# Alternating heavy and light experts, boundary tiles in pieces, the experts' sum in PSUM, light blocks in pairs

## The chip, the cores and the metric

The kernel runs on one NeuronCore of a Trainium2 chip. The core has TensorE (PE, matrix products, with its own weight loads), VectorE (DVE), ScalarE (ACT) and GpSimd (POOL); SyncE (SP) issues the weights' transfers from the chip's memory to 16 DMA engines. The metric is the time of one execution on the device in microseconds, the median of several runs. All numbers below are us unless marked otherwise.

## The reference

Two layers run over 256 tokens of width 1024. Each has a mixing sublayer (gated DeltaNet and MoBA attention, merged and projected by `w_o`) and a channel mixer: dense SwiGLU of width 2816 in layer 0, and in layer 1 eight SwiGLU experts of width 3584, of which each token uses two. After each sublayer the stream is normalised.

```python
mix = jnp.einsum('bsd,de->bse', g_a * y_a + g_b * y_b, w_o[layer])
x = _layer_norm(DEEPNORM_ALPHA * x + mix, ln1_g[layer], ln1_b[layer])
...
if layer % 2 == 0:
    ffn = _swiglu(x, ffn_w_gate[i], ffn_w_up[i], ffn_w_down[i])
else:
    ffn = _moe_swiglu(x, router_w[i], router_b[i], exp_w_gate[i], exp_w_up[i], exp_w_down[i])
x = _layer_norm(DEEPNORM_ALPHA * x + ffn, ln2_g[layer], ln2_b[layer])
...
for e in range(N_EXPERTS):
    y = y + gates[..., e:e + 1] * _swiglu(x, w_gate[e], w_up[e], w_down[e])
```

The last loop is that of `_moe_swiglu`; `gates` holds the softmax of each token's two largest router logits and is zero elsewhere. Everything is float32.

## The kernel before, in words

*Weights.* All large weights come in tiles of 128x2048 float32 (1 MB), in the order in which they are used. Class `Weights` loads a tile through SP (L76) into a raw slot, and splits it for PE into a high part `wh` (ACT, a copy to fp32r, L81) and a low part `wl` (DVE, raw minus high, L82); each has three buffers. The MoE phase has ten raw slots, among them `xhr`, `xlr`, `hbr`, `ohlr`, taken from tiles that are no longer used. A product is made as three matmuls per step of k (L205 to L207: high by high, low by high, high by low). A wait on a tile's conversion can be attached to a layer norm by `W.after`; `W.low` sends a tile's low half to another engine: at each of the three layer boundaries (`mix_out` of both layers, and `dense`) the next two tiles' low halves go to GpSimd.

*Boundaries.* The layer norm (`layer_norm_`, L236 to L260) runs for two halves of the tokens (c = 0, 1). For each half DVE makes statistics and two steps (L244, L245) per 512 columns, PE transposes the result (L250), and ACT and DVE write the transposed halves `xh` and `xl` (L253, L254). Ahead of the MoE the result is also kept untransposed as high and low part, `nat`: ACT L259, GpSimd L260. Behind it comes the router: PE L849, DVE L850 to L905, among which a rank of the experts by their number of tokens.

*Experts.* Each expert has 42 tiles: 28 for gate and up, two per block of 256 hidden units (14 blocks), and 14 for down. Tokens are gathered by matmuls with one-hot matrices (`onehot`, `gather`: PE L973, ACT L979, DVE L981), in groups of experts (0), (1, 2), (3, 4), (5, 6), (7), at the end of the last expert of the group before. A *heavy* expert holds up to 128 tokens and takes three matmuls per k (`tm`). A *light* one has up to 64: its high and low parts stand side by side in the 128 columns, so that two matmuls per k do (`tml`, L1027), and a fold by a matrix on PE (L1014) adds the halves. Three experts are heavy (the first three in order of their number of tokens), then five light ones.

A light block is worked on by `light_act`: ACT evicts the 128x512 result (L1011), PE folds (L1014, into `dl1`), ACT makes the silu (L1016), DVE the product (L1017, 128x128), ACT the high part (L1018), DVE the low part (L1019). A heavy block goes through `ffn_act` (L746 to L752, 128x256).

After the down product ACT and DVE make the gated result's high and low part (`ohl`, L1073, L1074), PE scatters it back to the tokens by one-hot matrices (L1079, L1080), and DVE adds it to `y` in four pieces of 128x512 (L1083), for all experts but the last, whose sum is made in PSUM with y.

*PSUM.* There are eight banks: `aux`, `mo`, `pm` twice each, `dl0`, `dl1` once. Gate and up results rotate through pm, pm, dl0; down uses the two of aux; gather, gates, one-hot transposes and the scatter use mo.

*Order.* A scheduler orders the instructions of each engine by the dependences and by the order of the code, with its own estimates; each engine then runs its list in order.

## Time and profile before

| | us |
|---|---|
| runs: median (lowest to highest of 3) | 1821.34 (1819.23 to 1824.04) |
| profiled execution | 1824.69 |
| its span | 1822.9 |
| PE busy in the span | 1738.2 |
| PE weight load | 1449.9 |
| DVE busy | 1389.8 |
| ACT busy | 1219.3 |
| POOL busy | 153.9 |

Busy times are sums over the span. Within it the mixing layers and the dense part take about the first half (the router ends near 890), and the eight experts follow, 101 to 126 us each. Which engine fills a stretch differs from stretch to stretch, so the share of the span says little by itself. An arrow behind a row in the views below, as in `[4.21 <-DVE res L245]`, tells how long the engine stood idle before that row, and what it waited for.

### The profile page before, as it was taken

What the parts mean: (1) busy time and instruction counts of PE and PEld (TensorE: products, weight loads), DVE (VectorE), ACT (ScalarE), POOL (GpSimd) and SP (SyncE); (2) the same over time, 40 slices, a digit from 0 to 9 for tenths busy, and PEclk for the clock granted to TensorE, in tenths of its full rate; (3) what the DMA queues carried; (4) which work ended last, traced back from release to release, by engine and by line L of the source; (5) the groups of instructions that cost most, each with busy time, mean ns of one, the idle gap of its engine ahead of it and who ended that gap; (6) DMA issues with size and microseconds to landing.
All of it is one profiled execution on the core that took longest, in us unless ns stands there. A gap on an engine that the chain in (4) does not pass through costs nothing.

```text
span 1822.9 us, 25299 instructions
## 1 busy us (share of the span) xinstructions
PE 1738.2 (95%) x9628; PEld 1449.9 (80%) x9628; DVE 1389.8 (76%) x1417; ACT 1219.3 (67%) x1363; POOL 153.9 (8%) x303
## 2 busy tenths in 40 slices
PE   8999999899989999999799999999999999999996
PEld 7988998788869888998678888888777767677774
DVE  5665556655455665547798888988999999999997
ACT  5676564444436656653477777777898889889895
POOL 0133200200020332201210000000000000000000
PEclk9999999999999999999799999999999999999998
DMA  8444334455544543337679999999999999999993
GB/s 274 169 147 137 113 131 177 178 184 185 184 162 162 165 152 115 110 116 289 265 276 346 350 352 369 347 362 348 391 410 410 414 411 408 421 394 421 418 407 126
DMA packets 100894, 492.13 MB, mean 270 GB/s; under 512 B 22099, under 2 KB 37916, under 8 KB 44060
## 3 DMA queue, kind: packets, MB, share of 16 engines
q1 hardware_dynamic: 72544, 475.91, 68.2%
q10 hardware_dynamic: 28220, 14.52, 2.9%
q8 instruction: 78, 1.28, 0.3%
q14 instruction: 52, 0.43, 0.1%
HBM read 484.61 MB, written 5.78 MB: 269 GB/s over the span
## 4 chain that ended last, share of the span: by engine, by line
PE 61%; DVE 15%; issue 7%; ACT 6%; POOL 6%; DMA 4%; ACTq 0%; DVEq 0%; SPq 0%; POOLq 0%
DVE wl L82 10%; PE pm L206 8%; PE pm L207 8%; PE pm L205 8%; ACT wh L81 4%; PE pm L1027 4%; PE aux L205 4%; PE aux L207 4%; PE aux L206 4%; POOL bLU L451 3%; POOL bT L449 3%; PE dl L1027 2%; PE dl L205 2%; PE dl L206 2%; PE dl L207 2%
## 5 line engine op out<-in xcount | busy, mean ns | idle before, releaser
L82 DVE TENSOR_TENSOR wl<-wraw,wh 128x2048 fp32r<-128x2048 f32 (+1 forms) x389 | 851.0, 2197 | 238.5 <-ACT wh L81 233.2
L81 ACT ACTIVATE wh<-wraw 128x2048 fp32r<-128x2048 f32 (+1 forms) x394 | 722.8, 1840 | 260.3 <-PE dl L207 48.5
L205 PE MATMUL pm<-xh,wh 128*128 128x256 f32 x896 | 263.2, 294 | 2.1 <-ACT wh L81 1.5
L207 PE MATMUL pm<-xh,wl 128*128 128x256 f32 x896 | 262.1, 293 | 1.1 <-DVE wl L82 1.1
L206 PE MATMUL pm<-xl,wh 128*128 128x256 f32 x896 | 262.3, 293 | 0.0
L205 PEld LDWEIGHTS pm<-xh,wh 128*128 128x128 f32 x896 | 172.5, 193 | 8.8 <-issue 4.8
L207 PEld LDWEIGHTS pm<-xh,wl 128*128 128x128 f32 x896 | 172.6, 193 | 6.2 <-issue 3.4
L206 PEld LDWEIGHTS pm<-xl,wh 128*128 128x128 f32 x896 | 172.5, 192 | 6.2 <-issue 4.8
L1027 PE MATMUL pm<-wl,xgh 128*128 128x512 f32 x376 | 157.2, 418 | 9.0 <-DVE wl L82 8.1
L1027 PE MATMUL pm<-wh,xgh 128*128 128x512 f32 x376 | 149.3, 398 | 0.4 <-ACT sg L1011 0.4
L1027 PE MATMUL aux<-wl,hb 128*128 128x512 f32 x280 | 106.9, 420 | 8.7 <-DVE wl L82 5.2
L1027 PEld LDWEIGHTS pm<-wl,xgh 128*128 128x128 f32 x376 | 70.9, 189 | 40.0 <-DVE wl L82 26.5
L1027 PE MATMUL aux<-wh,hb 128*128 128x512 f32 x280 | 99.3, 394 | 0.0
L206 PE MATMUL pm<-wl,xgh 128*128 128x512 f32 x224 | 90.5, 404 | 2.6 <-DVE wl L82 2.6
L205 PE MATMUL pm<-wh,xgh 128*128 128x512 f32 x224 | 91.9, 411 | 0.0
L207 PE MATMUL pm<-wh,xgl 128*128 128x512 f32 x224 | 89.8, 402 | 0.0
L1027 PEld LDWEIGHTS aux<-wl,hb 128*128 128x128 f32 x280 | 52.5, 187 | 43.9 <-DVE wl L82 34.3
L1027 PEld LDWEIGHTS pm<-wh,xgh 128*128 128x128 f32 x376 | 70.9, 189 | 13.9 <-ACT sg L1011 0.8
L1027 PE MATMUL dl<-wl,xgh 128*128 128x512 f32 x184 | 76.7, 417 | 5.2 <-DVE wl L82 4.8
L82 DVE TENSOR_TENSOR wl<-xhr,wh 128x2048 fp32r<-128x2048 f32 (+1 forms) x36 | 75.7, 2111 | 4.1 <-ACT wh L81 4.0
L1014 PEld LDWEIGHTS dl<-fold,sg 128*128 128x128 f32 x560 | 73.1, 191 | 6.0
L82 DVE TENSOR_TENSOR wl<-xlr,wh 128x2048 fp32r<-128x2048 f32 x32 | 73.3, 2289 | 4.1 <-ACT wh L81 3.6
(436 smaller groups left out, 3491.9 us busy)
## 6 DMA issues: line engine op xcount, KB each, us to landing
wraw<-in_w_exp SPq DMA_DIRECT2D x260, 1024.0 KB, 7.3
wraw<-in_w_mix SPq DMA_DIRECT2D x77, 1024.0 KB, 4.9
wraw<-in_w_ffn SPq DMA_DIRECT2D x33, 1024.0 KB, 4.8
xlr<-in_w_exp SPq DMA_DIRECT2D x33, 1024.0 KB, 7.2
xhr<-in_w_exp SPq DMA_DIRECT2D x32, 1024.0 KB, 7.1
LU<-zLU ACTq DMA_DIRECT2D x8, 512.0 KB, 3.9
hbr<-in_w_exp SPq DMA_DIRECT2D x4, 1024.0 KB, 10.9
wraw<-in_w_exp SPq DMA_DIRECT2D x12, 256.0 KB, 5.8
```

The source lines that it names most:

```text
L81: nc.scalar.activation(wh[:, c], raw[:, c], AF.Copy)
L82: (self.low.popleft() if self.low else nc.vector).tensor_sub(wl[:, c], raw[:, c], wh[:, c])
L205: pe.matmul(o, lh, rh, start=first, stop=False)
L206: pe.matmul(o, lh, rl, start=False, stop=False)
L207: return pe.matmul(o, ll, rh, start=False, stop=last)
L449: gp.tensor_mul(o, ab_[:, j, j + 1:16].unsqueeze(2).to_broadcast([32, n, j + 1]), lb[:, j:j + 1, 0:j + 1].to_broadcast([32, n, j + 1]))
L451: gp.tensor_sub(lb[:, j + 1:16, 0:j + 1], lb[:, j + 1:16, 0:j + 1], o)
L1014: pe.matmul(pt[:, j], ev[:, j], fold, start=True, stop=True)
L1027: pe.matmul(o, st(k0 + k), v[i][:, k, n0:n0 + 512], start=k0 + k == i == 0, stop=k0 + k == nk_all - 1 and i == 1)
```

## The change

1. The experts are taken as heavy, light, heavy, light, heavy, light, light, light. `PLACES` tells which rank stands at which place.
2. `W.low` becomes `W.pieces`: the two boundary tiles are converted by ACT and DVE in four pieces of 512 columns each, and none goes to GpSimd. `nat`'s low part goes from GpSimd to DVE, in two halves for each half of the tokens.
3. The sum over the experts is kept in four PSUM banks (`ys`: aux, aux, dl0, dl1) from the first expert to the last, and y is added to it at the last one; the additions at L1083 are gone.
4. For that, three banks (`pgb`: pm, pm, mo) serve gate/up, down and gather, and one bank of mo (`aux[0]`) serves folds, transposes, gates and one-hot transposes.
5. `light_act` folds each block as before, and does silu, product, high and low part once for two blocks.
6. The gather's casts of the low part go from DVE to ACT but for the first group; the gates and one-hot transposes move by some blocks.

```diff
-NHEAVY, LIGHT = 3, 64
+HEAVY, LIGHT = (0, 2, 4), 64
+PLACES = (1, 4, 2, 5, 3, 6, 7, 8)
...
+        cut = self.pieces.popleft() if self.pieces else parts
...
+        step = HB // cut
+        cols = [slice(i, i + step) for i in range(0, HB, step)]
...
                 nc.scalar.activation(wh[:, c], raw[:, c], AF.Copy)
-                (self.low.popleft() if self.low else nc.vector).tensor_sub(wl[:, c], raw[:, c], wh[:, c])
+                nc.vector.tensor_sub(wl[:, c], raw[:, c], wh[:, c])
...
-            gp.tensor_sub(nat[1][:, c], nx, nat[0][:, c])
+            for hf in range(2):
+                s = slice(hf * 512, (hf + 1) * 512)
+                dve.tensor_sub(nat[1][:, c, s], nx[:, s], nat[0][:, c, s])
...
-        W.low.extend([gp, gp])
+        W.pieces.extend([4, 4])
...
+        ys = [bank(t) for t in ("aux", "aux", "dl0", "dl1")]
+        pgb, aux = [bank("pm"), bank("pm"), bank("mo")], [bank("mo")]
...
-                        if part == 0:
-                            act.activation(dst, pt[:, :, i, s], AF.Copy)
+                        if part == 0 or g[0]:
+                            last = act.activation(dst, pt[:, :, i, s], AF.Copy)
...
-            pt = bank("dl1")[:, 0:4 * LIGHT].rearrange("p (j n) -> p j n", j=4)
+            pt = aux[0].rearrange("p (b j n) -> p b j n", b=2, j=4)
             for j in range(4):
-                pe.matmul(pt[:, j], ev[:, j], fold, start=True, stop=True)
-            sg = ev[:, 0].rearrange("p (a n) -> p a n", a=2)
-            silu = act.activation(sg, pt[:, 0:2], AF.Silu)
-            mul = dve.tensor_mul(sg, sg, pt[:, 2:4])
-            act.activation(ht[:, :, 0:LIGHT], sg, AF.Copy)
-            dve.tensor_sub(ht[:, :, LIGHT:], sg, ht[:, :, 0:LIGHT])
+                pe.matmul(pt[:, i % 2, j], ev[:, j], fold, start=True, stop=True)
+            if i % 2 == 0:
+                return last, last
+            ht = hb8[-1][:, (len(hb8) - 1) % 4]
+            sg = ev[:, 0:2].rearrange("p b (a n) -> p b a n", a=2)
+            silu = act.activation(sg, pt[:, :, 0:2], AF.Silu)
+            mul = dve.tensor_mul(sg, sg, pt[:, :, 2:4])
+            act.activation(ht[:, :, :, 0:LIGHT], sg, AF.Copy)
+            dve.tensor_sub(ht[:, :, :, LIGHT:], sg, ht[:, :, :, 0:LIGHT])
...
-                pg = bank(("pm", "pm", "dl0")[(e * nb + i) % 3])
+                pg = pgb[i % 3]
...
+            x_, po = pgb[(nb - 1) % 3], [pgb[nb % 3], pgb[(nb + 1) % 3]]
+            pgb = [x_] + po
             if e in last_of and e < NE - 1:
-                gather(groups[last_of[e] + 1])
+                gather(groups[last_of[e] + 1], aux + [x_])
...
-                    pt = ys[2 * c + n] if e == NE - 1 else bank("mo")
-                    pe.matmul(pt, PT[e][:, c], oh[:, n], start=e < NE - 1, stop=False)
-                    pe.matmul(pt, PT[e][:, c], ol[:, n], start=False, stop=True)
-                    if e < NE - 1:
-                        yc = y[:, c, n * 512:(n + 1) * 512]
-                        dve.tensor_add(yc, yc, pt)
+                    pt = ys[2 * c + n]
+                    pe.matmul(pt, PT[e][:, c], oh[:, n], start=e == 0, stop=False)
+                    pe.matmul(pt, PT[e][:, c], ol[:, n], start=False, stop=e == NE - 1)
```

Lines shift by a few in the changed kernel: L82 becomes L86, L205 to L207 become L209 to L211, L244, L245, L250 and L254 become L248, L249, L254 and L258, L674 becomes L680, L1017 and L1019 become L1032 and L1034.

VectorE's list at the first boundary, before, from the statistics of the first half of the tokens on (lnr, lnst, lnmv are the layer norm's, res its result):

```order
L238 BN_AGGR lnmv<-lnst 128x2
L244 SCALAR_TENSOR_TENSOR lnr<-lnr,lnmv,lngb 128x512 x2
L245 SCALAR_TENSOR_TENSOR res<-lnr,lnrs,lngb 128x512 x2
L674 SCALAR_TENSOR_TENSOR lnr<-xin,dl_3323 128x512
L236 BN_STATS lnst<-lnr 128x6
L254 TENSOR_TENSOR xl<-mo,xh 128x512
L238 BN_AGGR lnmv<-lnst 128x2
L254 TENSOR_TENSOR xl<-mo,xh 128x512
L244 SCALAR_TENSOR_TENSOR lnr<-lnr,lnmv,lngb 128x512 x2
L245 SCALAR_TENSOR_TENSOR res<-lnr,lnrs,lngb 128x512 x2
L254 TENSOR_TENSOR xl<-mo,xh 128x512 x2
L82 TENSOR_TENSOR wl<-wraw,wh 128x2048
```

And in the changed kernel, at the same place:

```order
L248 SCALAR_TENSOR_TENSOR lnr<-lnr,lnmv,lngb 128x512 x2
L249 SCALAR_TENSOR_TENSOR res<-lnr,lnrs,lngb 128x512 x2
L680 SCALAR_TENSOR_TENSOR lnr<-xin,dl_3323 128x512
L240 BN_STATS lnst<-lnr 128x6
L258 TENSOR_TENSOR xl<-mo,xh 128x512 x2
L242 BN_AGGR lnmv<-lnst 128x2
L86 TENSOR_TENSOR wl<-wraw,wh 128x512 x2
L248 SCALAR_TENSOR_TENSOR lnr<-lnr,lnmv,lngb 128x512 x2
L86 TENSOR_TENSOR wl<-wraw,wh 128x512 x2
L249 SCALAR_TENSOR_TENSOR res<-lnr,lnrs,lngb 128x512 x2
L753 TENSOR_TENSOR sg<-sg,pm 128x256
L258 TENSOR_TENSOR xl<-mo,xh 128x512 x2
```

The first of the two boundary tiles' pieces stand ahead of the first of these rows; those of the second now stand around the first steps of the second half's norm, and the first subtraction of a whole tile follows the second pair of xl.

PE's list around the transposes of the second half at the same boundary, before. The tiles wh_3385 and wl_3386 are the first boundary tile, wh_3445 the second; pm_3544 is the first block's result for the first half of the tokens, pm_3569 for the second half:

```order
L206 MATMUL pm_3544<-wl_3386,xh_69 128x512
L207 MATMUL pm_3544<-wh_3385,xl_3314 128x512
L205 MATMUL pm_3544<-wh_3445,xh_69 128x512
L250 MATMUL mo_3487<-cst_123,res_3390 128x128 x4
L250 MATMUL mo_3496<-cst_123,res_3390 128x128 x4
L205 MATMUL pm_3569<-wh_3385,xh_69 128x512
L206 MATMUL pm_3569<-wl_3386,xh_69 128x512
```

In the changed kernel (wh_3385 is the first tile, wh_3451 and wl_3452 the second, pm_3556 and pm_3581 the results for the two halves of the tokens):

```order
L209 MATMUL pm_3556<-wh_3451,xh_69 128x512
L210 MATMUL pm_3556<-wl_3452,xh_69 128x512
L211 MATMUL pm_3556<-wh_3451,xl_3314 128x512
L254 MATMUL mo_3499<-cst_123,res_3396 128x128 x4
L254 MATMUL mo_3508<-cst_123,res_3396 128x128 x4
L209 MATMUL pm_3581<-wh_3385,xh_69 128x512
L210 MATMUL pm_3581<-wl_3386,xh_69 128x512
```

Before, one matmul with the second tile stands ahead of the transposes, and the other 11 of that result stand behind them; in the changed kernel all 12 stand ahead.

VectorE's list in the gate and up part of a light expert, before:

```order
L82 TENSOR_TENSOR wl<-wraw_13699,wh 128x2048
L1017 TENSOR_TENSOR sg<-sg,dl_13729 128x128
L82 TENSOR_TENSOR wl<-wraw_13713,wh 128x2048
L1019 TENSOR_TENSOR hb<-sg,hb 128x2x64
L82 TENSOR_TENSOR wl<-wraw_13739,wh 128x2048
L1017 TENSOR_TENSOR sg<-sg,dl_13769 128x128
```

And in the changed kernel:

```order
L86 TENSOR_TENSOR wl<-wraw_9553,wh 128x2048
L86 TENSOR_TENSOR wl<-wraw_9567,wh 128x2048
L1032 TENSOR_TENSOR sg<-sg,mo 128x256
L86 TENSOR_TENSOR wl<-wraw_9587,wh 128x2048
L86 TENSOR_TENSOR wl<-wraw_9601,wh 128x2048
L1034 TENSOR_TENSOR hb<-sg,hb 128x4x64
```

Between a product and the low part stood one tile, and now two; the operations are twice as wide and half as many.

## Rows read from the trace of the kernel before

**Rows 1.** Stretches e1, e2, e5, e6: busy (count) PE, PEld, DVE, ACT, POOL; clock, DMA.

```profile
1023.00:1146.30 123.30, 123.30 (x554) 100.10 (x553) 109.00 (x78) 89.81 (x73) 0.00 (x0) 1.00 0.96 358
1146.30:1272.30 126.00, 126.00 (x574) 102.56 (x573) 111.32 (x89) 90.97 (x81) 0.00 (x0) 1.00 0.94 351
1486.00:1591.40 105.40, 100.35 (x468) 76.26 (x468) 103.07 (x77) 91.97 (x88) 0.00 (x0) 1.00 1.01 415
1591.40:1699.20 107.80, 102.82 (x489) 78.96 (x489) 104.32 (x82) 92.80 (x92) 0.00 (x0) 1.00 1.01 410
```

**Rows 2.** Waits of the DMA queue, light experts: total us, times, longest.

```profile
SPq L76 <- DVE hb L1019: 151.7, 68, 3.3
```

**Rows 3.** Timeline of ACT in e4: start, duration, line, operation, idle before.

```profile
1423.57 0.28 ACT L1016 ACTIVATE sg<-dl 128x128 f32<-128x128 f32 x1 [0.44 <-PE dl L1014]
1423.75 1.91 ACT L81 ACTIVATE wh<-xlr 128x2048 fp32r<-128x2048 f32 x1
...
1428.76 1.91 ACT L81 ACTIVATE wh<-wraw 128x2048 fp32r<-128x2048 f32 x1
```

**Rows 4.** Timeline of DVE in the experts: e0, e3, e4.

```profile
915.95 0.42 DVE L752 TENSOR_TENSOR hb<-dl,hb 128x256 fp32r<-128x256 f32 x1
916.28 0.41 DVE L747 TENSOR_TENSOR sg<-sg,dl 128x256 f32<-128x256 f32 x1
...
1358.97 6.69 DVE L82 TENSOR_TENSOR wl<-wraw,wh 128x2048 fp32r<-128x2048 f32 x3
1365.57 2.28 DVE L82 TENSOR_TENSOR wl<-xhr,wh 128x2048 fp32r<-128x2048 f32 x1
...
1383.71 1.28 DVE L1083 TENSOR_TENSOR y<-y,mo 128x512 f32<-128x512 f32 x2
1384.90 4.49 DVE L82 TENSOR_TENSOR wl<-wraw,wh 128x2048 fp32r<-128x2048 f32 x2
```

**Rows 5.** Timeline of DVE at the first boundary.

```profile
329.25 3.32 DVE L244 SCALAR_TENSOR_TENSOR lnr<-lnr,lnmv,lngb 128x512 f32<-128x512 f32 x2
...
336.40 1.41 DVE L244 SCALAR_TENSOR_TENSOR lnr<-lnr,lnmv,lngb 128x512 f32<-128x512 f32 x2
337.73 5.67 DVE L245 SCALAR_TENSOR_TENSOR res<-lnr,lnrs,lngb 128x512 f32<-128x512 f32 x2
```

**Rows 6.** Timeline of POOL at the first boundary.

```profile
337.12 5.05 POOL L82 TENSOR_TENSOR wl<-wraw,wh 128x2048 fp32r<-128x2048 f32 x1 [5.76 <-ACT wh L81]
```

**Rows 7.** Timeline of PE at the first boundary, then the stretch's busy times.

```profile
342.87 1.94 PE L250 MATMUL mo<-cst,res 128*128 128x128 f32 x8 [4.21 <-DVE res L245]
...
349.07 0.39 PE L206 MATMUL pm<-wl,xh 128*128 128x512 f32 x1
...
354.76 0.39 PE L205 MATMUL aux<-wh,xh 128*128 128x512 f32 x1
...
340.00:350.00 10.00, 7.13 (x23) 5.75 (x24) 7.07 (x5) 4.28 (x4) 2.18 (x1) 0.66 0.30 105
```

**Rows 8.** Timeline of PE at the second boundary.

```profile
542.60 1.94 PE L250 MATMUL mo<-cst,res 128*128 128x128 f32 x8 [4.74 <-DVE res L245]
...
555.56 0.28 PE L205 MATMUL pm<-xh,wh 128*128 128x256 f32 x1
```

**Rows 9.** Timeline of DVE at the second boundary.

```profile
536.36 5.44 DVE L244 SCALAR_TENSOR_TENSOR lnr<-lnr,lnmv,lngb 128x512 f32<-128x512 f32 x2
```

**Rows 10.** Timeline of DVE at the third boundary.

```profile
861.59 3.35 DVE L244 SCALAR_TENSOR_TENSOR lnr<-lnr,lnmv,lngb 128x512 f32<-128x512 f32 x2
...
869.20 2.83 DVE L245 SCALAR_TENSOR_TENSOR xin<-lnr,lnrs,lngb 128x512 f32<-128x512 f32 x1
...
872.68 0.21 DVE L855 TENSOR_TENSOR cmp<-lg 128x64 f32<-128x64 f32 x1
...
878.19 4.49 DVE L855 TENSOR_TENSOR cmp<-lg 128x64 f32<-128x64 f32 x1
```

**Rows 11.** DMA in the light experts: GB/s in 40 slices.

```profile
GB/s 354 388 395 424 421 415 389 423 419 420 381 399 422 420 418 390 424 418 397 396 424 417 422 423 420 421 417 366 385 422 422 419 421 422 418 402 389 422 421 377
```

More of the change, by code (lines that the diff above doesn't have):

```diff
@@ L54, in __init__ @@
         self.rings, self.n = [self.raw], 0
-        self.early, self.low = deque(), deque()
+        self.early, self.pieces = deque(), deque()
         self.tail = ()
@@ L724, in dense @@
             tail = [W.get() for _ in range(nt - 2)]
-            W.low.extend([gp, gp])
+            W.pieces.extend([4, 4])
             tail += [W.get(), W.get(False)]
@@ L913, in experts @@
         first, last_of = {g[0]: g for g in groups}, {g[-1]: i for i, g in enumerate(groups)}
-        light = lambda e: not base and e >= NHEAVY
+        light = lambda e: not base and e not in HEAVY
         cols = lambda e: [(spg if e == 0 else srt)[:, 2 * i:2 * i + 2] for i in range(3)]
@@ L926, in experts @@
             dve.tensor_scalar(iots[:, 1], iot, float(LIGHT), None, op0=ALU.add)
-            iota = lambda e: iots[:, 1 if e >= NHEAVY else 0]
+            iota = lambda e: iots[:, int(e not in HEAVY)]
         else:
@@ L941, in onehot, with gates @@
             return last
+        def gates(g):
+            n, pgs = len(g), aux[0]
+            for i, e in enumerate(g):
+                for c in range(2):
+                    pe.matmul(pgs[:, i:i + 1], P(e)[:, c].bitcast(F32), cols(e)[2][:, c, e:e + 1],
+                              start=c == 0, stop=c == 1)
+            dve.tensor_copy(gs[:, g[0]:g[0] + n], pgs[:, 0:n])
         def onehot_t(g):
-            pt = bank("mo")
-            pgs = bank("mo")
+            n, pt = len(g), aux[0]
             for i, e in enumerate(g):
@@ L967, in gather @@
                 for part, nat in ((0, nath), (1, natl)):
-                    pt = bank("aux" if g[0] == 0 and part else "mo")
-                    pt = pt[:, 0:n * 256].rearrange("p (k e n) -> p k e n", k=2, e=n)
+                    pt = free[turn % len(free)][:, 0:n * 256]
+                    turn += 1
+                    pt = pt.rearrange("p (k e n) -> p k e n", k=2, e=n)
                     for kk in range(2):
@@ L1040, in experts @@
                 if i:
-                    silu = hidden(pgs[i - 1], e)
+                    silu = hidden(pgs[i - 1], e, i - 1)
                 pgs.append(pg)
                 if e in first and i == 2:
+                    gates(first[e])
+                if e in first and i == 4:
                     onehot_t(first[e])
```

49 lines of the change are left out of this document (22 added, 27 removed).

## The prediction

> **What bounds the kernel now.** I read the busy times by stretch first, to see which engine fills each expert. A heavy expert is TensorE's: all 123.30 us of e1 are PE, and e2, with the gather for the next two, takes 126.00 [rows 1]. A light one is VectorE's: 103.07 of the 105.40 us of e5, with PE at 100.35 and ScalarE at 91.97; e6 has a gather and takes 107.80 [rows 1]. A busy PE is an upper bound here, since pipelined matmuls are drawn to their modelled ends: 25 matmuls of 512 columns in a full stretch go from 349.07 to 354.76, 0.228 us each [rows 7], so the 336 of a light expert need 77 us; with some 0.1 us for each of the other 132 of the 468 [rows 1] PE has work for 90 us.
>
> Second, the waits of the DMA queue: SyncE waits for VectorE to free a slot, 68 times on the small hb subtraction alone [rows 2]. So the weights' transfers are paced by VectorE, not the other way round.
>
> Third, the timelines of a light expert. ScalarE's conversions start at 1423.75 and 1428.76, so a block of two tiles takes 5.01 us; once a block ScalarE waits 0.44 us for PE's fold before the silu [rows 3]. VectorE, while nothing else stands between, spends 2.20 us per tile: three from 1358.97 to 1365.57 [rows 4]. Two blocks now take 10.02 us, of which four tiles are 8.80; the rest is four small operations and waiting.
>
> Fourth, the three layer boundaries, where VectorE makes the layer norm that PE waits for. There GpSimd takes one tile's low half in 5.05 us [rows 6], and VectorE's layer-norm steps last as long as it does: the same pair of steps takes 1.41 us at 336.40, 3.32 at 329.25, and the next pair 5.67 at 337.73 [rows 5]. PE then stands idle 4.21 us [rows 7].
>
> **The change part by part.** *Boundary pieces, first boundary.* GpSimd's two tiles go to VectorE, in four pieces of 512 columns. VectorE gets back 3.32 − 1.41 = 1.9 and 5.67 − 1.4 = 4.3, 6.2 us [rows 5]. It pays two tiles at some 2.4 (four pieces, 0.60 apart as the 512-column additions at 1383.71 are [rows 4]), 4.8 us. So the second half's norm is ready about 1.4 earlier and its transposes start at 341.5 instead of 342.87. The larger part is PE's order: ahead of these transposes stand 24 matmuls instead of 13, so that 11 that now come behind them (2.5 us) fill the gap. Behind them 35 matmuls lie today before the next block starts at 354.76 [rows 7]; 24 will. The transposes take 1.94 [rows 7], then 24 × 0.228 = 5.5: the next block starts at 348.9, 5.9 us earlier. In this I assume that the 24 run at 0.228; the granted clock is 0.66 in 340 to 350 today [rows 7], behind the idle gap, and with the gap nearly filled I expect little of that. If the low clock stays, 2 us of the 5.9 are lost.
>
> *Second boundary.* The same picture: 5.44 us for the pair at 536.36 [rows 9], idle 4.74 ahead of the transposes at 542.60 [rows 8]. VectorE gains as much as above, the transposes come at about 541.3; 1.9 and 5.5 behind them and 1.9 for the 16 small projections that stand in the same place give 550.6 for the next layer's first projection, 555.56 today [rows 8]: 5.0 us.
>
> *Third boundary.* VectorE gets back 1.9 at 861.59, some 2.1 at 869.20 (2.83 for one step of 0.7) and 4.3 at 878.19, where a comparison that takes 0.21 at 872.68 lasts 4.49, as long as GpSimd's subtraction [rows 10]. It pays 4.8 for the pieces and 2.4 for the four half-row subtractions of the natural layout that GpSimd did. Lower end 8.3 − 7.2 = 1.1, if nothing of that fits in VectorE's pauses for the router's matmuls. Upper end 6.5: the pauses hold all of it but what stands ahead of the second norm (4.3 plus 2.2). I take 3.7, the middle, since some pieces stand in a pause and some in the norm. The three boundaries: 5.9 + 5.0 + 3.7 = 14.6.
>
> *Expert sum in PSUM.* The four additions to y per expert go; for a light one they are VectorE's, 0.60 each [rows 4], on the engine that bounds it: 4 × 0.60 × 5 = 12.0. In the heavy experts they lie beside PE's work and bring nothing. PE's matmuls for the sum are the same ones.
>
> *Two blocks at a time.* For a pair VectorE has four tiles (8.80) and two operations on 128x256 instead of four on 128x128; such an operation takes 0.33 to the next start (915.95 to 916.28 [rows 4]). Lower end 9.46 us per pair, upper end today's 10.02, if the loop of three buffers from ScalarE over VectorE and PE and back holds the pace. I take 9.60: of the pauses today most come with the 0.44 us wait for the fold [rows 3], which now comes once per pair instead of twice, and VectorE is at 98% in e5. Seven pairs in five experts: 35 × 0.42 = 14.7.
>
> *The fewer banks.* Gate/up, down and gather share three banks, folds and transposes have one. I cost this at nothing: block i + 3 needs a bank whose eviction took place two blocks (some 9 us) before, and in PE's order a pair's first fold follows the last fold of the pair before it by 24 matmuls, 5.5 us, in which a silu and a product must be done. If that cover goes it is the last rival.
>
> *The order of experts.* It adds nothing up: three heavy, five light as before. But a gather lies on PE in a heavy expert (126.00 − 123.30 = 2.7) and on VectorE's path in a light one (107.80 − 105.40 = 2.4 to 2.6 [rows 1]); a second heavy one now has it and one light one less: −2.7 + 2.6 = −0.1. A heavy expert leaves VectorE idle, so raw slots fill before the next light one. Gather casts that go from VectorE to ScalarE I count at nothing.
>
> *Sum.* 14.6 + 12.0 + 14.7 − 0.1 = 41.2 us. The profiled execution took 1824.69, so 1783.5. The median of the runs lies 3.35 below that execution; the same gain from there would give 1780.1, which the range takes in.
>
> **A rule to weigh.** After the change a light expert should take 105.4 − 2.9 − 2.4 = 100.1 us, in which 42 tiles of 1.05 MB must come, 440 GB/s; the best slices of this trace show 424 [rows 11]. The Trainium skill, page "DMA: Bandwidth & Descriptors", section "Where 436 GB/s comes from", puts the fabric's ceiling at 435 GB/s, and says that for HBM to SBUF a limit of some 358 binds. The second figure is not what this trace shows; by the first a light expert could not stay under an estimated 101.2 us, and the sum would be up to 5.5 us smaller.
>
> **Rivals.** *Transfers bind.* At 424 GB/s a light expert takes 44.04 / 0.424 = 103.9 us, 3.8 more than I count: 5 × 3.8 = 19, time 1802.5. For it: the slices at 424 may be the ceiling. Against it: the waits of SyncE, and that three of the five follow a heavy expert, whose slots are full at the start; ten slots outlast the deficit of about 1.6 tiles in each.
>
> *The loop keeps its pace.* The pair still takes 10.02, because ScalarE or PE closes the loop, and only the additions are won: 1783.5 + 14.7 = 1798.2. For it: ScalarE waits on PE in each block [rows 3]. Against it: VectorE alone is busy 98% of e5, ScalarE only 87% [rows 1].
>
> *The pieces cost what the holding cost.* The boundaries give nothing, since VectorE's layer norm now carries two tiles itself: 1783.5 + 14.6 = 1798.1. For it: 6.2 against 4.8 is a small difference. Against it: the gain of PE's order doesn't depend on it. That the change doesn't do what it says at the boundaries (VectorE's steps are long for another reason than GpSimd's work) would show in the same place.
>
> *Slower: one bank for the pair.* Folds, silu and product share one bank. If the product stands behind two tiles on VectorE (4.7 us with the small ones), PE's next fold waits for it, and all matmuls behind it in order. PE has 100.1 − 90 = 10 us to spare per light expert, 1.5 per pair; the price is 4.7 − 1.5 = 3.2 for 35 pairs, 112 us, time 1895. It decides from 41.2 / 35 + 1.5 = 2.7 us of wait per pair on. Against it are the 24 matmuls between the folds.
>
> **How the numbers follow.** My forecast has 0.62; loop 0.12 (1798.2); pieces 0.10 (1798.1); transfers 0.10 (1802.5); one bank 0.03 (1895, or something over today); 0.03 for mixtures that leave no difference. The low end is pairs at 9.46 (4.9 more), the third boundary at its upper end (2.8 more) and the base of the median (3.4): 1783.5 − 11.1, 1772. The high end takes in the loop and the pieces and stops short of the transfers' full price: 1801. A measurement here tells about 0.3% from nothing, 5.5 us: all rivals but the last are faster. Faster 0.92, same 0.04, slower 0.04.
>
> **What would show it.** In the profile after: no subtraction of a tile on GpSimd, and the layer-norm pairs at 1.4 us each; PE's gap ahead of the second transposes under 1 us, with the granted clock near 1 behind it; ScalarE's conversions 4.80 us per block in a light expert, and 100 us for one without a gather, VectorE still over 95% busy. Wrong: SyncE or ScalarE waiting for transfers in light experts; PE waiting for the product ahead of a fold; VectorE's pieces late for PE at a boundary; pairs still at 10 us.

## The result, and the profile after

The changed kernel takes 1806.86 us (median of 5 runs, 1804.03 to 1809.39), the kernel before beside it 1819.23 (1818.81 to 1824.04): a ratio of 0.9926, 95% interval 0.9911 to 0.994, some 13 us less. The forecast was 1783.5, and its range ended at 1801. So the sign was right and the size was not: about a third of the 41 us came.

The busy line of the page after, engine by engine with the share of its span of 1807.6 us:

```profile
PE 1734.8 (96%) x9628; PEld 1454.6 (80%) x9628; DVE 1355.6 (75%) x1319; ACT 1221.1 (68%) x1339; POOL 119.1 (7%) x295
```

DVE has 34 us less to do than before (1389.8), POOL 35 less. Yet the light experts, which were DVE's, are hardly shorter. The stretches of five experts, columns as in [rows 1] (e1, e3, e5, e6 are light, e2 is heavy):

```profile
1018.00:1118.50 100.50, 98.97 (x477) 78.61 (x476) 98.66 (x61) 90.92 (x76) 0.00 (x0) 1.00 1.00 409
1118.50:1242.50 124.00, 124.00 (x565) 100.82 (x564) 107.58 (x76) 93.46 (x87) 0.00 (x0) 1.00 0.97 377
1242.50:1348.30 105.80, 101.44 (x478) 79.08 (x477) 99.67 (x61) 91.56 (x76) 0.00 (x0) 1.00 1.00 400
1472.60:1577.90 105.30, 101.01 (x477) 78.76 (x476) 99.59 (x61) 90.94 (x75) 0.00 (x0) 1.00 1.00 403
1577.90:1684.00 106.10, 101.71 (x490) 79.85 (x489) 100.52 (x61) 92.26 (x81) 0.00 (x0) 1.00 1.01 418
```

The first light expert takes the 100 us of the forecast; the others take 105 to 106, as before, though DVE's busy time fell from 103.07 to 99.59 in e5. The next table lists where each kernel's profiled execution spends its time. An expert is counted from the second gated copy on ACT (L1073 before, L1090 after) of the expert ahead to its own; e0 from its first matmul on `xgh`; the last to its first such copy. H is heavy, L light.

| us | before | after | alternation alone | heavy first | heavy first, bank freed | order set by code | the same, heavy first |
|---|---|---|---|---|---|---|---|
| e0 | 133.0 | 140.9 | 129.6 | 141.6 | 131.7 | 131.3 | 132.0 |
| e1 | H 123.3 | L 100.9 | L 116.2 | H 134.7 | H 126.4 | L 100.1 | H 125.9 |
| e2 | H 125.9 | H 124.0 | H 124.1 | H 127.1 | H 127.1 | H 124.0 | H 127.1 |
| e3 | L 105.6 | L 105.8 | L 105.2 | L 104.0 | L 103.8 | L 102.3 | L 103.1 |
| e4 | L 107.8 | H 124.4 | H 126.2 | L 107.4 | L 107.3 | H 124.4 | L 104.2 |
| e5 | L 105.6 | L 105.2 | L 105.7 | L 105.1 | L 105.1 | L 101.7 | L 101.6 |
| e6 | L 107.8 | L 106.1 | L 107.8 | L 106.3 | L 106.0 | L 102.7 | L 102.9 |
| e7 | L 105.3 | L 106.0 | L 105.3 | L 106.1 | L 105.9 | L 102.1 | L 102.4 |

The balance of the two profiled executions (1824.69 and 1809.39): the part ahead of the first norm +3.6 (it differs from execution to execution, see the last section); first norm to second 201.0 to 194.2, second to third 331.3 to 323.1, third norm to e0 33.87 to 31.23, together −17.6; e0 +7.9; the two heavy experts behind e0 −0.8; the five light ones 532.1 to 524.0, −8.1. That is −15.0 of the −15.3.

**The boundaries.** DVE at the first one; these rows answer to [rows 5]:

```profile
334.02 1.41 DVE L248 SCALAR_TENSOR_TENSOR lnr<-lnr,lnmv,lngb 128x512 f32<-128x512 f32 x2
335.35 1.41 DVE L249 SCALAR_TENSOR_TENSOR res<-lnr,lnrs,lngb 128x512 f32<-128x512 f32 x2
...
343.07 1.41 DVE L249 SCALAR_TENSOR_TENSOR res<-lnr,lnrs,lngb 128x512 f32<-128x512 f32 x2
```

PE there, and the stretch of [rows 7]:

```profile
343.97 1.28 PE L254 MATMUL mo<-cst,res 128*128 128x128 f32 x8
...
351.42 0.39 PE L209 MATMUL aux<-wh,xh 128*128 128x512 f32 x1
...
340.00:350.00 10.00, 9.94 (x47) 7.47 (x46) 8.53 (x12) 6.78 (x9) 0.00 (x0) 1.00 0.30 105
```

No step lasts 3.32 or 5.67 us any more, PE's 4.21 us of idle time ahead of the transposes are gone, and the granted clock is 1.00 where it was 0.66. From DVE's first addition of the norm to the next block it takes 351.42 − 327.41 = 24.0 us; before 354.76 − 323.83 = 30.9. At the third boundary the comparison that lasted 4.49 [rows 10] lasts 0.23:

```profile
867.09 0.23 DVE L861 TENSOR_TENSOR cmp<-lg 128x64 f32<-128x64 f32 x1
```

The Trainium skill, page "SBUF — State Buffer", section "SBUF: two separate sides", says that DVE and GpSimd share one port pair as an exclusive lock, which a DVE operation with two inputs from SBUF and a GpSimd operation that reads SBUF hold against each other for a whole instruction. The traces agree: 1.41 us without a GpSimd tile, 3.32 to 5.67 beside one; the pair of 5.67 us ends at 343.40, 1.2 us behind GpSimd's tile (337.12 + 5.05 = 342.17 [rows 5, 6]).

### The profile page after: what moved, and what is told of

It reads as the page before. It is cut to its first block, busy times and chain, and to the rows that moved or that the text cites. A ratio compares the mean times of both kernels' runs of the same rounds, so it can differ in the third digit from the quotient of the medians.

```text
span 1807.6 us, 25194 instructions
## 1 busy us (share of the span) xinstructions
PE 1734.8 (96%) x9628; PEld 1454.6 (80%) x9628; DVE 1355.6 (75%) x1319; ACT 1221.1 (68%) x1339; POOL 119.1 (7%) x295
## 4 chain that ended last, share of the span: by engine, by line
PE 64%; DVE 13%; issue 6%; POOL 6%; ACT 5%; DMA 4%; ACTq 0%; SPq 0%; DVEq 0%; POOLq 0%
DVE wl L86 10%; PE pm L211 9%; PE pm L209 9%; PE pm L210 9%; PE pm L1042 7%; ACT wh L85 4%; PE mo L1042 3%; POOL bLU L457 3%; POOL bT L455 3%; PE mo L210 3%; PE mo L211 2%; PE mo L209 2%; PE mo L1026 2%; PE aux L209 2%; PE aux L211 2%
## 5 line engine op out<-in xcount | busy, mean ns | idle before, releaser
L86 DVE TENSOR_TENSOR wl<-wraw,wh 128x2048 fp32r<-128x2048 f32 (+1 forms) x409 | 859.9, 2122 | 267.1 <-ACT wh L85 265.0
L85 ACT ACTIVATE wh<-wraw 128x2048 fp32r<-128x2048 f32 (+1 forms) x409 | 722.3, 1779 | 234.5 <-PE pm L210 49.9
L209 PE MATMUL pm<-xh,wh 128*128 128x256 f32 x896 | 263.9, 295 | 0.0
L211 PE MATMUL pm<-xh,wl 128*128 128x256 f32 x896 | 262.5, 293 | 0.3 <-DVE wl L86 0.3
L209 PEld LDWEIGHTS pm<-xh,wh 128*128 128x128 f32 x896 | 173.1, 193 | 6.8 <-issue 5.0
L211 PEld LDWEIGHTS pm<-xh,wl 128*128 128x128 f32 x896 | 173.2, 193 | 5.5 <-issue 3.4
L209 PE MATMUL pm<-wh,xgh 128*128 128x512 f32 x224 | 91.2, 407 | 0.0
L211 PE MATMUL pm<-wh,xgl 128*128 128x512 f32 x224 | 90.4, 404 | 0.0
L1042 PE MATMUL pm<-wl,hb 128*128 128x512 f32 x196 | 77.5, 415 | 6.5 <-DVE wl L86 4.7
L1042 PEld LDWEIGHTS pm<-wh,xgh 128*128 128x128 f32 x376 | 70.9, 189 | 14.6 <-ACT wh L85 0.7
L86 DVE TENSOR_TENSOR wl<-xlr,wh 128x2048 fp32r<-128x2048 f32 (+1 forms) x36 | 75.8, 2110 | 8.3 <-ACT wh L85 8.0
L86 DVE TENSOR_TENSOR wl<-xhr,wh 128x2048 fp32r<-128x2048 f32 (+1 forms) x36 | 75.7, 2108 | 4.5 <-ACT wh L85 4.5
L1026 PEld LDWEIGHTS mo<-fold,sg 128*128 128x128 f32 x560 | 73.1, 191 | 6.7 <-ACT hot L964 0.6
L1042 PE MATMUL mo<-wl,xgh 128*128 128x512 f32 x184 | 75.6, 411 | 2.6 <-DVE wl L86 2.3
L1042 PE MATMUL pm<-wh,hb 128*128 128x512 f32 x196 | 73.1, 393 | 0.5 <-ACT wh L85 0.5
L1042 PE MATMUL mo<-wh,xgh 128*128 128x512 f32 x184 | 73.4, 399 | 0.0
```

The lines of the kernel that those rows point to most:

```text
L85: nc.scalar.activation(wh[:, c], raw[:, c], AF.Copy)
L86: nc.vector.tensor_sub(wl[:, c], raw[:, c], wh[:, c])
L209: pe.matmul(o, lh, rh, start=first, stop=False)
L211: return pe.matmul(o, ll, rh, start=False, stop=last)
L1026: pe.matmul(pt[:, i % 2, j], ev[:, j], fold, start=True, stop=True)
L1042: pe.matmul(o, st(k0 + k), v[i][:, k, n0:n0 + 512], start=k0 + k == i == 0, stop=k0 + k == nk_all - 1 and i == 1)
```

## The experiments

**One part at a time, on the kernel before.** First the boundary pieces alone, then the order of the experts alone:

```
pieces:  - self.low.popleft() ... gp.tensor_sub(wl, ...)   + four dve.tensor_sub of 128x512
order:   - NHEAVY = 3             + HEAVY = (0, 2, 4); PLACES = (1, 4, 2, 5, 3, 6, 7, 8)
```

> The kernel before with only the boundary pieces: no tile's low half on GpSimd, four pieces on ScalarE and VectorE for the two tiles of each boundary, the natural low part on VectorE. Theory (the boundaries bring what they bring in the changed kernel, 6.8, 7.9 and 4.8 us, and the first expert keeps its 132 us): 15 to 19 us less than before, 1800 to 1804. Rival (the first expert gives some 8 us of it back, since it starts on tiles that are converted later): 8 to 11 us less, 1808 to 1811.

> The kernel before with only the alternating order of heavy and light experts. Theory (heavy and light experts cost what they cost in any order, a gather costs 2.5 us in either): within 3 us of before, 1816 to 1822. Rival (a light expert behind a heavy one starts with full raw slots and runs faster, as the first light one of the changed kernel does): 5 us for each of the two that newly stand behind a heavy one, 1809 to 1812.

The pieces took 1804.47 us, ratio 0.9915 (0.989 to 0.994): by themselves all of what the change gained. The alternation alone took 1829.68, 1.0046 (1.0029 to 1.0063): slower, which neither the theory nor the rival had. The loss stands in the first light expert, 116.2 us, where ScalarE's eviction waits for a buffer of `sg` that DVE's low half (L1020) frees late, and PE's folds wait for the eviction:

```profile
1073.65 0.60 ACT L1012 ACTIVATE sg<-pm 128x512 f32<-128x512 f32 x1 [2.53 <-DVE hb L1020]
```
```profile
1074.30 1.97 PE L1015 MATMUL dl<-fold,sg 128*128 128x64 f32 x8 [4.42 <-ACT sg L1012]
```

So the rest of the change, 1806.86 against 1804.47, was worth about nothing, and something in it must cost what its additions save.

**The bank of e0.** PE's idle rows in the first blocks of e0, after; then what ACT and DVE do ahead of the last:

```profile
918.64 0.50 PE L210 MATMUL pm<-wl,xgh 128*128 128x512 f32 x1 [1.93 <-DVE wl L86]
923.38 0.44 PE L756 MATMUL mo<-cst,sg 128*128 128x128 f32 x2 [1.91 <-DVE hb L758]
940.09 0.69 PE L756 MATMUL mo<-cst,sg 128*128 128x128 f32 x2 [4.44 <-DVE hb L758]
```
```profile
931.50 0.36 ACT L964 ACTIVATE hot<-mo 128x256 fp32r<-128x256 f32 x1
...
935.46 1.91 ACT L85 ACTIVATE wh<-wraw 128x2048 fp32r<-128x2048 f32 x1 [0.83 <-PE mo L211]
937.28 0.36 ACT L757 ACTIVATE hb<-mo 128x256 fp32r<-128x256 f32 x1
```
```profile
937.40 2.29 DVE L86 TENSOR_TENSOR wl<-wraw,wh 128x2048 fp32r<-128x2048 f32 x1 [0.45 <-ACT wh L85]
939.61 0.42 DVE L758 TENSOR_TENSOR hb<-mo,hb 128x256 fp32r<-128x256 f32 x1
```

The one bank `mo` held the one-hot transposes (L962), then a block's transposed hidden values. Their copy waits behind a conversion on ACT, the low half behind a tile on DVE, and PE's next transposes wait 4.44 us for that. Behind that wait the granted clock is at 0.50 for 5 us:

```profile
940.00:945.00 5.00, 4.91 (x13) 3.91 (x14) 1.11 (x4) 0.66 (x2) 0.00 (x0) 0.50 0.75 303
```

Before, two banks held these, and only one wait of 2.58 us stood in e0. The first experiment moves the gates and one-hot transposes of e0 ahead of the bank's other use; the second also puts GpSimd's making of y (L1064) into the code of e2:

```
e0bank:  - if e in first and i == 2: gates      + i == (2 if e else 0)
         - if e in first and i == 4: onehot_t   + i == (4 if e else 0)
e0y:     - if e == base == 0 and i == nb - 2:   + if e == 2 and base == 0 and ...
```

> The changed kernel with one edit: the gates and the transposed one-hot of the first expert are made behind its first block instead of behind its third and fifth, when the one bank for folds and transposes isn't used otherwise. Theory (in the first expert the one-hot transposes stand in the same bank between two blocks' transposes, so that PE waits 4.44 and 1.91 us for VectorE's low part, the clock falls behind the longer wait, and the expert takes 8 us longer than before): the first expert's end comes 5 to 8 us earlier against the router's end, 1799 to 1802. Rival (the first expert is longer because its tiles arrive or are converted later after the shorter boundary): within 2 us of the changed kernel's 1806.9.

> The first expert's edit as before, and GpSimd's addition of the two halves into y moved from the first expert to the end of the third's gate and up part. Theory (the addition holds VectorE's subtraction for 6.4 us instead of 2.2, PE waits 2.36 us for it in the first expert, and in the third VectorE is far enough ahead): 2 us less than the run with the first edit alone (1799.0), 1797. Rival (the third expert pays the same): 1799.

With the bank free: 1798.98 us, 0.9881 (0.9844 to 0.9917), e0 takes 131.9 us instead of 140.9, and of PE's three waits one is left:

```profile
916.65 0.50 PE L210 MATMUL pm<-wl,xgh 128*128 128x512 f32 x1 [2.36 <-DVE wl L86]
```

That is the 8 us. The second edit gave 1795.88 (0.9831 to 0.9884), with an overlapping interval, and its profile has the same times. It moved y in the code only: the scheduler still has GpSimd make it in e0, at 909.78 us (909.83 in `e0bank`), so that this run measures `e0bank` a second time and says nothing about the place of y:

```profile
909.78 4.62 POOL L1064 TENSOR_TENSOR y<-nat,nat 128x2048 f32<-128x2048 f32 x1 [174.53 <-DVE wl L86]
```

**Why the light experts stay at 105.** One pair of blocks on ACT in e1 (L1023 evicts a block, L1031 is the silu, L1033 the high part, L85 converts a weight tile), then in e3:

```profile
1071.66 0.58 ACT L1023 ACTIVATE sg<-pm 128x512 f32<-128x512 f32 x1
1072.33 1.92 ACT L85 ACTIVATE wh<-xlr 128x2048 fp32r<-128x2048 f32 x1
1074.15 0.57 ACT L1023 ACTIVATE sg<-mo 128x512 f32<-128x512 f32 x1
1074.63 0.37 ACT L1031 ACTIVATE sg<-mo 128x256 f32<-128x256 f32 x1
1075.32 3.73 ACT L85 ACTIVATE wh<-wraw 128x2048 fp32r<-128x2048 f32 x2 [0.32 <-PE pm L1042]
1078.95 0.40 ACT L1033 ACTIVATE hb<-sg 128x256 fp32r<-128x256 f32 x1
...
1084.07 0.37 ACT L1031 ACTIVATE sg<-mo 128x256 f32<-128x256 f32 x1
```
```profile
1282.96 0.60 ACT L1023 ACTIVATE sg<-pm 128x512 f32<-128x512 f32 x1
1283.45 1.91 ACT L85 ACTIVATE wh<-xhr 128x2048 fp32r<-128x2048 f32 x1
1286.62 0.39 ACT L1031 ACTIVATE sg<-mo 128x256 f32<-128x256 f32 x1 [1.26 <-PE mo L1026]
1286.90 1.91 ACT L85 ACTIVATE wh<-wraw 128x2048 fp32r<-128x2048 f32 x1
1288.70 0.59 ACT L1023 ACTIVATE sg<-mo 128x512 f32<-128x512 f32 x1
...
1296.85 0.39 ACT L1031 ACTIVATE sg<-mo 128x256 f32<-128x256 f32 x1 [1.25 <-PE mo L1026]
```

In e1 the silu stands behind the eviction of the next pair's first block: by then PE has folded, nothing waits, and a pair takes 1084.07 − 1074.63 = 9.44 us. In e3 it stands one place earlier, waits 1.25 us for PE's fold, and the next conversion stands behind it; a pair takes 1296.85 − 1286.62 = 10.23. ACT is far from full (91.56 of 105.80), but its list is run in order, and DVE waits for the conversion that stands behind the wait:

```profile
1287.81 0.41 DVE L1032 TENSOR_TENSOR sg<-sg,mo 128x256 f32<-128x256 f32 x1
1288.84 2.29 DVE L86 TENSOR_TENSOR wl<-wraw,wh 128x2048 fp32r<-128x2048 f32 x1 [0.62 <-ACT wh L85]
```

Nothing in the code sets this: the same lines come out in one order in e1 and in the other in the four experts behind it. The experiments: the silu of a pair one block later; more buffers instead (four for `wh`, `wl`, paid for with two raw slots); the later silu with e0's bank freed and the evictions put behind one or two more conversions.

```
late:   + if pend: with tc.issue_after(last.ins): act_pair(*pend.pop())   # behind the next eviction
moe4:   + every fourth tile: wh4, wl4 (fourth buffers), depth 3, raw slots 8 instead of 10
late3:  late, e0bank and  + with tc.issue_after(W.acts[-1 - i % 2].ins): act.activation(ev, ...)
```

In `late` and `late3` the one-hot work of light experts overwrites one or two pairs' folds in the shared bank, so part of the values are others; the instructions are the same ones.

> The changed kernel with one edit: in a light expert the silu, product, high and low part of a pair come one block later, behind the next block's eviction on ScalarE. In the changed kernel the first light expert has this order by itself and takes 9.45 us per pair (100.9 us in all), the other four have the silu one conversion earlier, wait 1.25 us there in each pair and take 10.23 us (105.2 to 106.5 in all). Theory (ScalarE's silu stands in its queue ahead of a conversion and waits for PE's fold, and so holds up the loop of three buffers): the four also come to 9.5 us per pair and some 100.5 us, about 18 us less than the changed kernel's 1806.9, so near 1789. Rival (transfers: the first light expert starts with full slots, and the later ones are held to what arrives, 400 to 418 GB/s): the order changes nothing, 1805 to 1809, and ScalarE or SyncE wait for transfers instead. Second rival (PE now waits for the product ahead of the next pair's first fold): 10 us per pair or more, 1807 or slower.

> The changed kernel with four buffers instead of three for the high and for the low half in the experts (and loads up to three tiles ahead), paid for with two of the ten raw slots. Theory (the loop of three buffers is what holds a light pair at 10.2 us): 9.5 us per pair in all light experts, 100 to 101 us each, about 18 us less than the changed kernel: 1788 to 1790. Rival (transfers bind, and the slots matter): 1806 or slower. Rival (the order in ScalarE's queue, which stays as the scheduler makes it): within 4 us of 1806.9.

> The changed kernel with the first expert's gates and one-hot transposes behind its first block (as in the run before), the second stage of a light pair one block later, and the evictions of a light expert's blocks each put behind one or two more conversions in ScalarE's queue, which is the order that the first light expert of the changed kernel has by itself. The second stage alone left 9.8 us per pair, and evictions that wait 0.4 to 1.3 us for PE ahead of a conversion. Theory (ScalarE's queue order closes the loop of three buffers): the four later light experts take 67 to 68 us for gate and up instead of 71.9, some 101 us each, 16 to 18 us less than the run with the first expert's edit alone (1799.0): 1781 to 1784. Rival (transfers: the later light experts are held to 400 to 420 GB/s): 1793 or more, with waits for transfers on ScalarE. Rival (buffers, not order): 9.8 us per pair stays, 1795 to 1798.

`late` took 1803.06 (0.9843 to 0.9929) where 1789 was expected: the silu's wait is gone, but a pair takes 9.82 us in e3 and not 9.5; light experts from e3 on fell to 103.8 to 105.1. `moe4` took 1805.13: the light experts from e3 on stay at 105.2 to 106.0 and their pairs at 10.23, and SyncE's waits for transfers from 1250 us on are 5.9 us in all, so what the loop lacks isn't buffers. (Its first light expert takes 106.0 instead of 100.9, and e0 138.4.) `late3`, with e0's bank freed as well, took 1789.74 (0.9802 to 0.9857) where 1781 to 1784 was expected, light experts at 101.3 to 104.5, most pairs still at 9.82. So the silu's place is worth 0.41 of the 0.79 us between the two orders; the rest had to come from the places of the other operations.

**The order set by code.** The last version puts evictions, folds, silu and high part between the weight conversions in the order of e1, in all light experts; the gates and one-hot work stand in the down part, and y's making in e2's code (it still runs in e0, at 911.90):

```
- if e in first and i == 2: gates(first[e])          (inside the blocks, bank mo)
+ if e and e in first and i == 4: gates(...), onehot_t(..., x_)        (down part)
+ if i % 2 and i > 1 and hb == 0:                    (behind the first tile of an odd block)
+     odd, _ = evict(pgs[i - 2], i - 2); folds(odd, i - 2)
+ if i % 2 and hb:                                   (behind the second tile)
+     even, last = evict(pgs[i - 1], i - 1)          (next pair's first block)
+     if i > 1: silu = product(odd)                  (silu and product of the pair before)
+     folds(even, i - 1)
+ if i % 2 == 0 and i > 3 and hb: halves(*silu[2:])  (high and low part)
```

> All five light experts with the order that the first one of the changed kernel has: ScalarE's queue per pair is conversion, eviction, conversion, eviction, silu, conversion, conversion, high part, conversion, set by the code. Folds and products are those of the changed kernel. Gates and one-hot transposes come in the down part (the first expert's behind its first block), GpSimd's addition in the third expert. Theory (the place of evictions, silu and high part in ScalarE's queue decides whether the loop of three buffers holds VectorE up): a pair takes 9.45 to 9.55 us in every light expert, a light expert 100 to 101; against the run with the first expert's edit and the moved addition (1795.9) some 4 to 5 us in each of four, 1776 to 1780. Rival (the slots: the light experts that don't stand behind a heavy one, the seventh and the eighth, are held by transfers): 1785, with those two at 104 to 106. Rival (a pair cannot go under 9.8 us outside the first light expert for a reason in PE): 1790 or more.

It took 1782.56 us (1780.34 to 1784.61), ratio 0.9797 (0.976 to 0.9834): 38 us under the kernel before, 24 under the changed one, some 8 of them by e0's bank. Light experts take 100.1 to 102.7. Two of its stretches, e3 and e5:

```profile
1231.50:1333.80 102.30, 100.74 (x481) 78.66 (x480) 99.49 (x60) 91.21 (x75) 0.00 (x0) 1.00 1.00 412
1458.20:1560.00 101.80, 100.23 (x476) 78.23 (x475) 99.29 (x60) 90.69 (x74) 0.00 (x0) 1.00 1.00 411
```

DVE's busy time in e5, 99.29, is nearly the 99.59 of the changed kernel; what went is the rest of the stretch, from 5.7 us to 2.5. Two silus of e3, one pair apart:

```profile
1270.66 0.39 ACT L1032 ACTIVATE sg<-mo 128x256 f32<-128x256 f32 x1 [0.75 <-PE mo L1025]
...
1280.27 0.39 ACT L1032 ACTIVATE sg<-mo 128x256 f32<-128x256 f32 x1 [0.75 <-PE mo L1025]
```

A pair takes 9.61 us there, and 9.42 in e1. So the order on ACT is what held the four later experts at 10.23. The last 0.2 us, which leave the time 2.6 above the expected range, are not explained; the silu still waits 0.75 us.

**What the additions and the pair are worth.** Four additions of 128x512 on DVE are put back into each expert but the last, in the changed kernel and in the version above (they add the gated result unscattered, so y has other values); and light blocks are worked on one at a time again, on the one bank:

```
adds, pairsadds:  + dve.tensor_add(yc, yc, oh[:, n])   (behind each scatter product)
singles:          - pt = aux[0] for two blocks   + pt = aux[0][:, 0:256] for each block
```

> The changed kernel with four additions of 128x512 put back on VectorE behind each expert but the last, as many and as large as those that the change took away; they add the gated result into y instead of the experts' sum, so that the output is another. Theory (in the four later light experts the loop through ScalarE's queue sets the pace and VectorE has 0.6 to 1 us of pauses per pair): less than 4 us over the changed kernel's 1806.9. Rival (by the prediction's working, each light expert pays 2.4 us): 12 us, 1819.

> The kernel with the set order in all light experts, and the same four additions put back on VectorE (the output is another for the same reason). Theory (with the order mended VectorE is what bounds a light expert, so its work counts): 8 to 12 us more than that kernel without them. Rival (VectorE still has pauses): under 4 us.

> The changed kernel with the light blocks worked on one at a time again, all else as changed. By the prediction's working (VectorE's work sets the pace): a pair costs 0.4 us more in five experts, 14.7 us, 1821. By the theory that the loop of three buffers sets it: the pair brought nothing in the four later light experts, whose pairs take 10.23 us against 10.02 before; within 4 us of 1806.9, or less, since the additions are gone and a single block's wait is short.

`adds`: 1815.04 us, 8.2 more than the changed kernel; neither the 4 at most nor the 12 of the rival. In the profiles the five light experts pay 7.1 and the two heavy ones 1.1 each. The pairs keep their 10.23 us, since the additions stand where one expert ends and the next begins. With the additions back, the light experts take 531.2 us, against 532.1 before the change: the rest of the change, two blocks at a time, fewer banks and the alternation, brought 0.9 there.

`pairsadds`: 1796.79, 14.2 more than the version without, where 8 to 12 was expected. But that isn't the price of the additions alone. The light experts pay 7.9, hardly more than in `adds`; 5.5 stand in the heavy e2. There GpSimd now does make y, which it does in e0 in every other version, and VectorE's subtraction beside it takes 6.35 us:

```profile
1106.78 8.64 POOL L1077 TENSOR_TENSOR y<-nat,nat 128x2048 f32<-128x2048 f32 x1 [374.51 <-DMA wraw<-in_w_exp]
...
1111.21 6.35 DVE L87 TENSOR_TENSOR wl<-wraw,wh 128x2048 fp32r<-128x2048 f32 x1
```

So these two runs don't show that an addition costs more once the order is mended.

`singles`: 1898.44 us, ratio 1.0421, 91 over the changed kernel, where 1821 or no difference was expected; its light experts take 115.7 to 129.3 us. Its waits from 1050 to 1800 us (total us, times, longest):

```profile
DVE wl L86 <- ACT wh L85: 83.1, 73, 5.3
ACT sg L1023 <- DVE hb L1031: 30.9, 30, 3.1
PE mo L1026 <- ACT sg L1023: 27.2, 7, 4.6
```

PE waits for the eviction, the eviction for DVE's low half, which frees one of the two buffers of `sg`, and DVE for a conversion that stands behind the eviction on ACT. In the changed kernel the two blocks at a time keep it out of this knot. That the one bank ties it is not shown: the kernel before folds one block at a time in one bank too (`dl1`) and has no such wait of PE over 2 us, and the alternation alone has the same knot on `dl1` (the 4.42 us above). e6, which has no gates or one-hot work in the bank, takes 115.7 us all the same.

**The order of the experts.** Three heavy ones first, as before the change, in the changed kernel; the same with the bank freed ahead of e0 and e1; the same in the version with the order set by code:

```
noalt, pairsnoalt:  - HEAVY = (0, 2, 4); PLACES = (1, 4, 2, 5, 3, 6, 7, 8)   + (0, 1, 2); (1, ..., 8)
noaltbank:          noalt and   + h = 0 if e < 2 else 2   (gates at block h, one-hots at 2 * h)
```

> The changed kernel with the order of experts as before the change: three heavy, then five light ones. Theory (a heavy and a light expert cost the same in any order, and the scheduler gives the good order of ScalarE's queue to the first light expert wherever it stands, the second order to the four others): within 4 us of the changed kernel's 1806.9, with one light expert at about 101 us and four at 105 to 106. Rival (the alternation fills the slots and lets the light experts run faster): the light experts behind light ones take 1 us or more longer each, 1811 or more.

> The changed kernel with the order heavy, heavy, heavy, then the five light ones (as before the change), and with the gates and one-hot transposes of experts 0 and 1 moved ahead of those experts' first activation, so that the one bank never holds two things at once in a heavy expert. Without that move the same order took 1824.1 us, 17 more than the changed kernel; there expert 1 took 134.7 us where a heavy expert takes 124, with 4.4 us waits of PE at L756 for DVE in it, as expert 0 had. Theory 'shared bank': the heavy order loses because the second group's gates and transposes then fall into a heavy expert: both experts get their 8 us back, 1824 - 8 - 8 to 10 = 1806 to 1808, expert 1 at 124 to 126. Rival 'alternation itself': the alternating order is worth the 17 us by its transfers (SP is kept waiting less); then only expert 0's 8 us come back, 1815 to 1817, and expert 1 stays above 131.

> The version with the queue order of light experts set by code (measured at 1782.6 us), with the order heavy, heavy, heavy, then the five light ones. Its gates and transposes stand at expert 0's block 0 and in the down parts. Theory 'shared bank': alternation is worth only what the heavies lose behind heavies, 1 to 6 us: 1783 to 1789. Rival 'alternation itself' : worth about 13 or more: 1795 to 1800, with the added time in the heavies 1 and 2 (over 130 us each) or in waits of SP's queue for data.

`noalt` took 1824.14 us, 17 over the changed kernel, where 4 at most were expected. Its e1 takes 134.7 us, and PE has e0's wait a second time:

```profile
1074.98 0.46 PE L756 MATMUL mo<-cst,sg 128*128 128x128 f32 x2 [4.44 <-DVE hb L758]
```

The gates and one-hot work of the second group now lie in a heavy expert; in the alternating order they lie in a light one. With the bank freed in both the kernel took 1806.89 (0.9905 to 0.9952): e0 and e1 got back 9.9 and 8.3 us, as that theory has it. That leaves 0.9928 against 0.9881 of `e0bank`, 8.6 us, and `pairsnoalt` at 1792.35 (0.9825 to 0.9883) against 0.9797, 10.4 us, for the alternation itself; here the expectation was too small. (The intervals of each pair overlap a little, the runs don't, and the stretches e1 to e7 are 9.0 and 10.0 us longer.) In the profiles of the last pair the heavy e1 and e2 hold 4.6 of it (253.0 against 248.4 for two) and the light ones 5.4. In a heavy expert behind another, of the version with the freed bank, PE waits at the head of the down part:

```profile
1092.10 0.50 PE L210 MATMUL pm<-wl,hb 128*128 128x512 f32 x1 [1.10 <-DVE wl L86]
...
1099.52 0.50 PE L210 MATMUL pm<-wl,hb 128*128 128x512 f32 x1 [0.97 <-DVE wl L86]
```

The light experts' part lies in the first two, 103.1 and 104.2 us against 100.1 and 102.3 (the second has a gather, which in the alternating order a heavy one has). And where light experts follow light ones in the version with the order set by code, the queue begins to wait for transfers (from 1270 us on, heavy first; then the same row with the order alternating):

```profile
SPq L79 <- DMA wraw<-in_w_exp: 34.4, 46, 2.1
```
```profile
SPq L79 <- DMA wraw<-in_w_exp: 8.1, 8, 2.1
```

How much of the light experts' 5.4 us is due to that wasn't separated: the version with the freed bank loses 4 us there as well, with 1.3 us of such waits.

## Why the prediction was wrong

**Boundaries, right.** 14.6 us were forecast, 17.6 came in the profiles and 16 in the runs of the pieces alone. The mechanism was the one named: steps back at 1.41, PE's gap filled by the order, clock at 1.00 behind it. The first gave 6.8 for 5.9, the second with what follows 6 to 8 for 5.0, the third 2.6 for 3.7.

**Two blocks at a time, the step that failed.** For the light experts 26.7 us were forecast (14.7 for the pairs, 12.0 for the additions), and 8.1 came, of which the additions are 7.1. "I take 9.60" should have been 10.23 in four of five light experts. The reason given was that the wait for the fold would come once per pair instead of twice. It does come once, but lasts 1.25 us, not 0.44, since the silu stands where PE can't yet have folded. That wait is about half of the loss: with it gone, in `late`, a pair takes 9.82, and the places of the evictions and of the high part hold most of the rest. The prediction read ACT's share (87% in e5) as room. A queue that runs in order has no room at the place where it waits. ScalarE's list tells which places those are, and e1 and e3 differ in it; I priced them alike. The value itself was to be had: 9.44 in e1, and 9.61 in the others in the version with the order set by code.

**The additions, too high.** 12.0 forecast, 8.2 measured on the changed kernel. Three light experts pay 1.4 to 1.8 us and the first 2.2, where 2.4 was counted, and the last pays nothing; the heavy ones, counted at nothing, pay 1.1 each. With the mended order the light experts pay about the same, so that the failed step isn't the reason; why the price is lower stays open.

**The banks at nothing, wrong in another place.** I looked at the light experts and found the cover of 24 matmuls; there it held (PE waits 0.2 us at a fold in all experts behind e0). The bank is also used by e0's gates and one-hot work among heavy blocks, which the prediction didn't look at: 7.9 us.

**The order at −0.1, wrong in size.** Alone on the kernel before it costs 8 us, through the wait for `sg` in the first light expert; in the changed kernel it is worth 17, 8 of them by keeping the second group's one-hot work out of a heavy expert.

**The rivals.** "The loop keeps its pace" is what happened, and it had 0.12; its 1798.2 plus e0's 7.9 is 1806.1. That this is the measured time is in part chance, since the boundaries gave 3.0 more than forecast, the additions 3.8 less, and the part ahead of the first norm took 3.6 more in that execution. "One bank" didn't happen in the light experts; `singles` is as slow as that rival, but by another knot. "Transfers bind" didn't show in the changed kernel: SyncE still waits on DVE alone in e6, for instance 51.5 us for `wl`:

```profile
SPq L78 <- DVE wl L86: 51.5, 28, 3.1
```

At the pace of the version with the order set by code it starts to: there e6 moves 420 GB/s, and with the heavy experts first e4 to e6 move 421. The Trainium skill, page "DMA: Bandwidth & Descriptors", section "Where 436 GB/s comes from", names 435 GB/s for the fabric and some 358 as the limit for loads from HBM; the measured 421 is above the second, which doesn't hold here, and just under the first.

## What to carry to other kernels

Before an engine with idle time is counted as cover, read the order of its list at the place where it waits: what stands behind the wait is late, however low its share. Where fewer banks serve more uses, price every user of a bank, also the rare ones at the start of a phase. Give an order that matters to the code: two experts from the same lines came out with different orders, and the difference was 5 us. And look up in the profile whether an edit moved what it was meant to move: y stayed in e0 in the run that was to move it.

## What was not expected of the hardware

PE waits at one place ahead of the first norm in both kernels, 2.46 us after and 2.35 before, with the same instructions around it. In after's execution the granted clock was at 0.50 (the lower of the two levels, 1.2 GHz) behind it, in before's it stayed at 1.00. The stretch behind the wait, after and then before:

```profile
180.00:185.00 5.00, 5.00 (x20) 4.32 (x19) 2.88 (x5) 0.38 (x1) 0.00 (x0) 0.50 0.51 151
```
```profile
180.00:185.00 5.00, 5.00 (x38) 4.19 (x37) 3.23 (x4) 2.61 (x3) 0.00 (x0) 1.00 0.41 108
```

In this stretch 20 matmuls ran instead of 38, and the first norm began 3.6 us later (327.41 against 323.83). The change isn't the cause, nor is the length of the wait: the code there is the same, and `pairsadds`, with a wait of 2.46 us at that place, has 1.00 behind it, `late`, with 2.29, 0.50. Over the profiles of all versions the norm begins between 320.9 and 332.2, which is why times were compared here from norm to norm and from expert to expert. What decides the clock there is not known.
